# Three transformer blocks on one core: the two halves of the tokens run half a stage apart, and the split weights go through DRAM

## The chip, the cores and the metric

The kernel runs on one core of a Trainium2 chip. The metric is the time of the whole program on the device in microseconds, as the median of repeated runs. Beside it there is one execution that was profiled, whose trace the rows below come from.

## What is computed

512 tokens of 1024 channels go through three blocks in fp32, ten stages in all:

```python
x = first_block(x, c, ...)    # swiglu, hybrid mixer (gMLP + forgetting attention), swiglu, each modulated by c
x = second_block(x, ...)      # swiglu, RWKV-7 recurrence + 31-tap convolution, swiglu
x = third_block(x, ...)       # twice: mixer (top-256 attention + differential attention), swiglu
```

A swiglu is `(silu(h @ w_gate) * (h @ w_up)) @ w_down` with an inner width of 2816. Every mixer begins with projections `h @ w_in` and ends with `@ w_out`. Before each stage stands an RMS norm; in the first two blocks another stands behind it.

## The kernel before, in words

**Halves.** The tokens are two halves of 256, `hf` 0 and 1. Each stage is written out for half 0 and then for half 1 (line 1479). Channels lie on partitions. The second half needs the first half's keys, values, running sums and recurrent state of the same mixer, and nothing else of it.

**Weights.** fp32 products are made of three fp16 matmuls (`three`, line 382). A weight slot is 128 x 1024 fp32, eight 128 x 128 tiles. `Weights.slot` (line 356) loads it by SP into one of three staging buffers `st`, ScalarE writes the high half into a ring buffer `wr`, VectorE the rest (lines 360 to 363). The ring has 12 buffers. A slot is split once and read by both halves: `W(name)` (line 377) keeps one object per matrix, so the buffer is free again when the second half has used it. There are 524 slots. A slot feeds 24 matmuls of 256 columns in each half; the projections to token rows use tile `pt` with 512 columns.

**Order.** The order on every engine is fixed when the program is built. A list scheduler takes, among what is ready, the smallest priority number. That number is a virtual time per half, `vt[hf]`, which `adv` (line 267) advances by each piece's TensorE time, plus `lag[hf]`. The first half has lag 0; the second has `LAGS` of the stage (16 to 30 us), set in its norm (line 451). `boost` makes work earlier, `later` makes it later; attention is boosted by 80 us. The lag is in one half's own TensorE time.

**Stages.** A feed-forward (`ffn`, line 510) makes 22 groups of 16 tiles for gate and up (tile `pgu`, 1056 matmuls a half), then a down-projection of 8 groups (tile `po`, 528). Mixer 1 (line 686) and mixer 3 (line 1227) have projections `pp`, softmax tiles `ps` and an output `po<-mix`. Mixer 2 (line 858) has a recurrence in four chunks: `correction` (line 1057) is a chain of products in tile `pT`, `chunk` (line 1090) a chain through `pA`, `pxy`, `pu` and `psp`; the second half starts from the state that the first leaves. Convolution taps run on VectorE beside it (line 941). The modulation of block one is summed on VectorE from w_ada (`ada_row`, line 558), beside the first feed-forwards.

**GpSimd** clears 20 buffers (`hl`, line 645) and issues no transfer.

Of the kernel before, what the change touches and what calls it, by code (L numbers as in the profile page):

```python
# [243 lines left out]
def tile_three_blocks(ctx: ExitStack, tc: tile.TileContext, d, col_at, con_at, out, phases=None):  # L244
# [107 lines left out]
    class Weights:  # L352
        def __init__(self, name):
            self.name, self.src, self.have = name, d[name], {}

        def slot(self, s):
            if s not in self.have:
                with boost(CB if self.name == "gu10" and s < 3 else WBS.get(self.name, WB)):
                    st = stage.tile([128, 1024], F32, name="st", tag="st")
                    nc.sync.dma_start(out=st, in_=self.src[s])  # L360
                    r = ring.tile([128, 2, 1024], F16, name="wr", tag="wr")
                    S.activation(r[:, 0], st, AF.Copy, scale=WS)  # L362
                    V.scalar_tensor_tensor(r[:, 1], st, WS, r[:, 0], op0=OP.mult, op1=OP.subtract)  # L363
                self.have[s] = r
            return self.have[s]
# [10 lines left out]

    def W(name):
        if name not in weights:
            weights[name] = Weights(name)
        return weights[name]  # L380

# [128 lines left out]
    def ffn(hf, gu, dn, pre, bias, post, key):  # L510
        hh = prenorm(hf, pre, bias, key)
        acts = []
        for n in range(NF):
            adv(hf, 5.23)
            if n % 2 == 0:
                acts.append(m2k(hf, [128, 2, 2, TH], F16, "act"))
            act = acts[-1]
            p = pmm(hf, [128, 2, TH], name="pgu")
            gemm(p[:, 0], W(gu), 16 * n, KD, pair(hh))
            gemm(p[:, 1], W(gu), 16 * n + 8, KD, pair(hh), bank=False)  # L520
            with boost(EB):
                t = t1k(hf, name="fth")
                S.activation(t, p[:, 0], AF.Tanh, scale=0.5 / WS)  # L523
                V.scalar_tensor_tensor(t, t, 1.0, p[:, 0], op0=OP.add, op1=OP.mult)  # L524
                a = t1k(hf, name="fac")
                V.scalar_tensor_tensor(a, t, 0.5 / WS / WS / AS, p[:, 1], op0=OP.mult, op1=OP.mult)  # L526
                split(hf, act[:, 0, n % 2], act[:, 1, n % 2], a)
            beside(key, hf, n)
        x = lambda k: (acts[k // 2][:, 0, k % 2], acts[k // 2][:, 1, k % 2])
        if post is None:  # L530
            out_add(hf, W(dn), NF, x, AS / WS)
# [7 lines left out]
        acc = out_tiles(hf, W(dn), NF, x, y, AS / WS, key)  # L539
        postnorm(hf, acc, y, post)  # L540

# [144 lines left out]
    def mixer1(hf):  # L686
# [24 lines left out]
        for j in range(8):  # L711
            adv(hf, 2.6)
            p = pmm(hf, [128, TH], name="pp")
            gemm(p, W("m1_qk"), (j + 4) % 8 * KD, KD, px)
            with boost(MB):
# [31 lines left out]
        for tt in range(2):  # L747
            vt_ = kv2k(hf, name="v")
            token_gemm(hf, W("m1_v"), hh, tt, lambda p: S.activation(vt_, p, AF.Copy, scale=1.0 / WS))
            m1["v", hf].append(vt_)  # L750
# [26 lines left out]
        for j in range(4):  # L777
            adv(hf, 2.6)
            p = pmm(hf, [128, TH], name="pp")
            gemm(p, W("m1_u"), j * KD, KD, px)  # L780
            if j % 2 == 0:
# [8 lines left out]
        for tt in range(2):  # L790
            g = m2k(hf, name="vg")

            def ev(p, g=g):
                for q in range(2):
                    gelu(hf, g[:, q * 256:(q + 1) * 256], p[:, q * 256:(q + 1) * 256])
            token_gemm(hf, W("m1_g"), hh, tt, ev)
            bn = tiny(hf, 6, "bn")
# [35 lines left out]
        y = lambda m: ys[m // 2][:, m % 2]  # L833
        acc = out_tiles(hf, W("m1_o"), KD, pair(mix), y, 1.0 / WS)
        postnorm(hf, acc, y, one_col(gpost, 8))
# [22 lines left out]
    def mixer2(hf):  # L858
# [36 lines left out]
        for j in order:  # L895
            adv(hf, 2.6)
            p = pmm(hf, [128, TH], name="pp")
            gemm(p, W("m2_s"), j * KD, KD, px)
            with boost(BOOST["m2r"]):
# [19 lines left out]
        def gate_units(j):  # L919
            adv(hf, 5.2)  # L920
            p = pmm(hf, [128, 2, TH], name="pgl")
            gemm(p[:, 0], W("m2_c"), 16 * j, KD, px)
            gemm(p[:, 1], W("m2_c"), 16 * j + 8, KD, px, bank=False)
            with boost(GB):
# [294 lines left out]
        y = lambda m: ys[m // 2][:, m % 2]  # L1219
        acc = out_tiles(hf, W("m2_o"), KD, lambda k: (mix[:, k, 0], mix[:, k, 1]), y, 1.0 / WS)  # L1220
        postnorm(hf, acc, y, lambda k: col("mpost2", k))
# [5 lines left out]
    def mixer3(hf, l):  # L1227
# [24 lines left out]
        def rotated(w, i0, dst, tab, scale):  # L1252
            adv(hf, 2.6)
            p = pmm(hf, [128, TH], name="pp")
            gemm(p, W(w), i0 * KD, KD, px)
            with boost(RB):
# [83 lines left out]
        for tt in range(2):  # L1340
            t = kv2k(hf, name="vb")
            token_gemm(hf, W(f"m3_vb{l}"), hh, tt, lambda p: S.activation(t, p, AF.Copy, scale=1.0 / WS))
            vb.append(t)
# [38 lines left out]
        for tt in range(2):  # L1382
            t = kv2k(hf, name="va")
            token_gemm(hf, W(f"m3_va{l}"), hh, tt, lambda p: S.activation(t, p, AF.Copy, scale=1.0 / WS))
            va.append(t)
# [3 lines left out]
        with boost(BOOST["m3a"]):  # L1389
# [19 lines left out]
        out_add(hf, W(f"m3_o{l}"), KD, pair(mix), 1.0 / WS)  # L1409

# [90 lines left out]
```

## Time and profile before

| | us |
|---|---|
| median of 3 runs (3500.28 to 3503.44) | 3501.31 |
| the profiled execution | 3507.87 |
| its span, first to last instruction | 3506.0 |
| TensorE busy | 3309.1 (94%) |
| VectorE busy | 2171.3 (62%) |
| ScalarE busy | 1545.5 (44%) |

The 16 DMA engines moved 327.89 MB, a mean of 94 GB/s; 28.1% of their time went to the loads' queue. The mean granted TensorE clock was 0.98 of full speed. Stages can be told in the trace by the names of tiles: mixer 1 lies between about 336 and 720 us of the span, mixer 2 between 1320 and 1860, the two layers of mixer 3 between 2100 and 2520 and between 2760 and 3180; each stretch has some feed-forward work of its neighbours in it. A count of matmuls can be short by a few, since some records are missing.

### The profile page before, as it was taken

To read this page: it belongs to the slowest core of one execution; us is meant where nothing else is said; L and a number is where in the kernel's file an instruction comes from. 1 tells how busy PE (TensorE), PEld (TensorE's weight loads), DVE (VectorE), ACT (ScalarE), POOL (GpSimd) and SP (SyncE) were. 2 spreads that over 40 slices of the span, in tenths; PEclk is the share of its full clock that TensorE was granted. 3 is DMA by queue.
4 is the path that set the end of the run, shared out by engine and by line. 5 is a ranking of instruction groups with operands and counts; after the bars stand their busy time and mean duration, and the time that the engine had idled before them with its cause. 6 is when DMAs were issued, how large, how long until landed. Compare 5 with 4: busy or idle time off the path is not lost. (4 is left out here: it accounts for less than half of the span.)

```text
span 3506.0 us, 71986 instructions
## 1 busy us (share of the span) xinstructions
PE 3309.1 (94%) x30164; PEld 2815.7 (80%) x30164; DVE 2171.3 (62%) x5240; ACT 1545.5 (44%) x3335; POOL 19.1 (1%) x24
## 2 busy tenths in 40 slices
PE   5999999999999999997789999889999998999998
PEld 5888867788888888886678887667888876688887
DVE  8953768844374437688884438887544488855433
ACT  3332466433343324424243326886433278853331
POOL 0000000000000000000000000000000000000000
PEclk9999999999999999987889999999999999999999
DMA  8932313232323332201023323112233321123331
GB/s 276 326 110 91 118 55 130 67 103 97 99 96 102 104 97 91 70 5 34 4 89 104 102 97 99 55 43 67 85 104 102 105 85 51 41 80 109 103 99 47
DMA packets 105591, 327.89 MB, mean 94 GB/s; under 512 B 12584, under 2 KB 18088, under 8 KB 105008
## 3 DMA queue, kind: packets, MB, share of 16 engines
q1 hardware_dynamic: 105264, 323.28, 28.1%
q8 instruction: 236, 3.87, 0.5%
q14 instruction: 91, 0.75, 0.1%
HBM read 321.14 MB, written 2.10 MB: 92 GB/s over the span
## 5 line engine op out<-in xcount | busy, mean ns | idle before, releaser
L314 PEld LDWEIGHTS <-wr 128*128 128x128 f16 x24000 | 2351.0, 99 | 327.8 <-issue 25.5
L314 PE MATMUL pgu<-hh,wr 128*128 128x256 f16 x12672 | 1402.6, 273 | 7.9 <-ACT wr L362 2.3
L363 DVE SCALAR_TENSOR_TENSOR wr<-st,wr 128x1024 f16<-128x1024 f32 x524 | 640.3, 1223 | 353.3 <-ACT wr L362 344.0
L314 PE MATMUL po<-act,wr 128*128 128x256 f16 x6336 | 702.0, 273 | 0.1
L362 ACT ACTIVATE wr<-st 128x1024 f16<-128x1024 f32 x524 | 552.2, 1055 | 323.2 <-PE pgu L314 128.3
L314 PE MATMUL pp<-hh,wr 128*128 128x256 f16 x3072 | 384.1, 274 | 4.8 <-DVE rot L1261 2.2
L523 ACT ACTIVATE fth<-pgu 128x256 f32<-128x256 f32 x264 | 101.3, 384 | 590.4 <-PE pgu L314 590.2
L524 DVE SCALAR_TENSOR_TENSOR fth<-fth,pgu 128x256 f32<-128x256 f32 x264 | 111.0, 420 | 355.9 <-ACT fth L523 355.8
L314 PE MATMUL po<-mix,wr 128*128 128x256 f16 x1536 | 198.0, 282 | 15.9 <-ACT mix L444 9.0
L444 ACT ACTIVATE act<-fac 128x256 f16<-128x256 f32 x264 | 110.2, 417 | 174.1 <-DVE fac L526 173.8
L314 PE MATMUL pt<-wr,hh 128*128 128x512 f16 x576 | 145.4, 383 | 1.6 <-DVE wr L363 1.6
L445 DVE TENSOR_TENSOR act<-fac,act 128x256 f16<-128x256 f32 x264 | 111.3, 422 | 50.5 <-ACT act L444 50.0
L492 DVE TENSOR_TENSOR acc<-acc,sq 128x256 f32<-128x256 f32 x84 | 35.4, 421 | 149.5 <-ACT sq L491 149.5
L1260 ACT ACTIVATE rsw<-pp 32x256 f32<-32x256 f32 x304 | 114.3, 376 | 19.6 <-PE pp L314 15.3
L432 ACT ACTIVATE sq<-x 128x256 f32<-128x256 f32 x154 | 56.5, 411 | 134.0 <-DVE x L501 129.6
L526 DVE SCALAR_TENSOR_TENSOR fac<-fth,pgu 128x256 f32<-128x256 f32 x264 | 110.8, 420 | 7.7
L485 ACT ACTIVATE y<-po 128x256 f32<-128x256 f32 x64 | 24.5, 383 | 204.8 <-PE po L314 204.7
L941 DVE SCALAR_TENSOR_TENSOR mix<-glu,cols,mix 128x256 f32<-128x256 f32 x240 | 102.2, 477 | 0.1
L314 PEld LDWEIGHTS <-hh 128*128 128x128 f16 x768 | 62.2, 100 | 48.3 <-issue 3.2
L619 DVE TENSOR_REDUCE amx<-ps 128x1 f32<-128x128 f32 (+3 forms) x160 | 77.3, 487 | 34.4 <-PE ps L314 32.6
L565 DVE SCALAR_TENSOR_TENSOR ada<-adw,csil,ada 128x512 f32<-128x512 f32 x126 | 91.0, 747 | 5.8 <-DMA adw<-in_w_ada_dram 5.6
L501 DVE SCALAR_TENSOR_TENSOR x<-po,x 128x256 f32<-128x256 f32 x64 | 26.9, 422 | 108.1 <-PE po L314 108.0
(356 smaller groups left out, 2935.6 us busy)
## 6 DMA issues: line engine op xcount, KB each, us to landing
st<-in_gu_dram SPq DMA_DIRECT2D x264, 512.0 KB, 3.5
st<-in_dn_dram SPq DMA_DIRECT2D x132, 512.0 KB, 3.5
adw<-in_w_ada_dram SPq DMA_DIRECT2D x144, 256.0 KB, 5.2
st<-in_m_o_dram SPq DMA_DIRECT2D x32, 512.0 KB, 3.6
st<-in_m_b_dram SPq DMA_DIRECT2D x16, 512.0 KB, 3.6
st<-in_m_a_dram SPq DMA_DIRECT2D x16, 512.0 KB, 3.8
st<-in_m_s_dram SPq DMA_DIRECT2D x14, 512.0 KB, 3.6
st<-in_m_qk_dram SPq DMA_DIRECT2D x8, 512.0 KB, 4.0
```

The source lines that it names most:

```text
L314: return PE.matmul(out_, lhsT=l, rhs=r, start=start, stop=stop, skip_group_check=True)
L362: S.activation(r[:, 0], st, AF.Copy, scale=WS)
L363: V.scalar_tensor_tensor(r[:, 1], st, WS, r[:, 0], op0=OP.mult, op1=OP.subtract)
L444: S.activation(hi, src, AF.Copy)
L445: V.tensor_tensor(lo, src, hi, op=OP.subtract)
L523: S.activation(t, p[:, 0], AF.Tanh, scale=0.5 / WS)
L524: V.scalar_tensor_tensor(t, t, 1.0, p[:, 0], op0=OP.add, op1=OP.mult)
L526: V.scalar_tensor_tensor(a, t, 0.5 / WS / WS / AS, p[:, 1], op0=OP.mult, op1=OP.mult)
L565: V.scalar_tensor_tensor(ada_acc[g, h], src, csil[:, k:k + 1], ada_acc[g, h], op0=OP.mult, op1=OP.add)
L619: V.tensor_reduce(nm, s[:, :nk], axis=AX.X, op=OP.max, negate=True)
L941: V.scalar_tensor_tensor(cc(j), gl[:, i:i + TH], dw[:, j * 31 + i:j * 31 + i + 1], cc(j), op0=OP.mult, op1=OP.add)
L1260: S.activation(sw[a:a + 32], p[c:c + 32], AF.Copy, scale=scale)
```

## The change

The lag of the second half becomes 90 us in every stage but the first, whose lag grows by 8 us with each of the eight groups of its down-projection (`WIDEN`). Since a slot can't wait so long in the ring, each half has its own object for a matrix: the first half splits a slot as before, and GpSimd stores the split slot (512 KB, 4 KB a row) to a DRAM buffer `aw...` of its own; the second half loads it by SP from there straight into a ring buffer, without staging and without splitting. `gu10` alone, the first gate and up, is shared as before (`TOGETHER`). The modulation sums of group 8 use the other half's buffers.

```diff
-LAGS = {"f10": 26, "m1": 16, "f11": 22, "f21": 26, "m2": 22, "f22": 24,
-    "m30": 30, "f30": 22, "m31": 30, "f31": 18}
+LAGS = {"f10": 26, "m1": 90, "f11": 90, "f21": 90, "m2": 90, "f22": 90,
+    "m30": 90, "f30": 90, "m31": 90, "f31": 90}
+WIDEN = {"f10": 8}
+TOGETHER = ("gu10",)
...
+    away = pool("away", 1, space=bass.MemoryType.DRAM)
...
+        def __init__(self, name, before=None):
+            self.name, self.src, self.have, self.kept, self.before = name, d[name], {}, {}, before
...
+                    if self.before:
+                        r = ring.tile([128, 2, 1024], F16, name="wr", tag="wr")
+                        nc.sync.dma_start(out=r, in_=self.before.kept[s])
+                    else:
+                        st = stage.tile([128, 1024], F32, name="st", tag="st")
+                        nc.sync.dma_start(out=st, in_=self.src[s])
+                        r = ring.tile([128, 2, 1024], F16, name="wr", tag="wr")
+                        S.activation(r[:, 0], st, AF.Copy, scale=WS)
+                        V.scalar_tensor_tensor(r[:, 1], st, WS, r[:, 0], op0=OP.mult, op1=OP.subtract)
+                        if self.name not in TOGETHER:
+                            self.kept[s] = away.tile([128, 2, 1024], F16, name=f"aw{self.name}_{s}")
+                            nc.gpsimd.dma_start(out=self.kept[s], in_=r)
...
+    def W(name, hf):
+        key = name, hf if name not in TOGETHER else 0
+        if key not in weights:
+            weights[key] = Weights(name, weights[name, 0] if key[1] else None)
+        return weights[key]
...
             beside(key, hf, NF + m)
+            if hf and key in WIDEN:
+                lag[1] += WIDEN[key]
             adv(hf, nk * 0.327)
...
-            ada_acc[g, h] = kv2k(0, name="ada")
+            ada_acc[g, h] = kv2k(g // 8, name="ada")
```

The built order moves with it. On SP, where block one's last feed-forward (`gu11`, `dn11`) is followed by block two's first (`gu21`), the loads stood like this before:

```order
L360 DMA st_10030<-in_dn11_dram 128x1024
L360 DMA st_10059<-in_dn11_dram 128x1024
L360 DMA st_10093<-in_dn11_dram 128x1024
L360 DMA st_10122<-in_dn11_dram 128x1024
L360 DMA st_12230<-in_gu21_dram 128x1024
L360 DMA st_12259<-in_gu21_dram 128x1024
```

and now:

```order
L370 DMA st_10423<-in_dn11_dram 128x1024
L370 DMA st_10454<-in_dn11_dram 128x1024
L370 DMA st_12696<-in_gu21_dram 128x1024
L370 DMA st_12727<-in_gu21_dram 128x1024
L370 DMA st_12766<-in_gu21_dram 128x1024
L367 DMA wr_10621<-awgu11_0_8157 128x2048
L367 DMA wr_10647<-awgu11_1_8188 128x2048
```

All 66 slots of the first half's stage are loaded, then three of its next stage, then all 66 of the second half's stage from the kept copies, then the rest of the first half's next stage. On TensorE the first half's 1056 gate and up matmuls and 301 of its down-projection stand ahead of the second half's first gate matmul, in each of the five stages with kept gate and up weights; between them stand 12 + 192 (`m1_g`, `m1_o`), 254 (`dn11`), 62 + 192 (`m2_c`, `m2_o`), 14 + 192 and 11 + 192 (mixer 3) matmuls of the second half's stage before, with 44, 8, 759, 243 and 243 small ones.

On TensorE at the end of the first half's recurrence in mixer 2 (`psp` and `pxy` of its last chunk), before, `pT<-zb` being the second half's first correction:

```order
L314 MATMUL psp<-uv,bkt 64x64 x8
L314 MATMUL pxy<-uv,aat 64x64 x7
L314 MATMUL pw<-low,wau 128x128
L314 MATMUL pw<-kr,masks 128x128
L314 MATMUL pw<-low,gup 128x256 x2
L314 MATMUL pw<-low,wau 128x128
L314 MATMUL pw<-low,gup 128x256 x2
L314 MATMUL pw<-low,wau 128x128
L314 MATMUL pw<-kr,masks 128x128
L314 MATMUL pT<-zb 64x64 x6
```

and now:

```order
L317 MATMUL psp<-uv,bkt 64x64 x8
L317 MATMUL pxy<-uv,aat 64x64 x7
L317 MATMUL pw<-low,gup 128x256 x4
L317 MATMUL nst<-ones,acc 128x2 x2
L317 MATMUL nbc<-ndg,ones 128x128 x2
L1207 MATMUL pch<-ident,yt 128x128 x6
L317 MATMUL nst<-ones,acc 128x2 x2
L1207 MATMUL pch<-ident,yt 128x128 x2
L317 MATMUL pmu<-csum,ones 128x256
L317 MATMUL nbc<-ndg,ones 128x128 x2
L317 LDWEIGHTS wr
L317 MATMUL po<-mix,wr 128x256
```

Before, the second half's chain follows at once, with no dense matmul between the two chains; now 1096 dense matmuls stand between them. Within the first chain there were 156 by the trace and by the order, and there are 94; within the second 168, and there are 252.

On GpSimd the memsets of `hl` had the queue to themselves; now 480 stores stand there, and the memsets among them:

```order
L376 DMA awdn_20_2828<-wr 128x2048
L376 DMA awdn_21_2859<-wr 128x2048
L661 MEMSET hl 64x1024 x2
L376 DMA awm_qk_5033<-wr 128x2048
L376 DMA awm_qk_5069<-wr 128x2048
```

A store waits for the split of its slot, and for the eighth store ahead of it.

## Rows read from the trace of the kernel before

**Rows 1.** The page, its first line and part 1: busy us, share, instructions.

```profile
span 3506.0 us, 71986 instructions
PE 3309.1 (94%) x30164; PEld 2815.7 (80%) x30164; DVE 2171.3 (62%) x5240; ACT 1545.5 (44%) x3335; POOL 19.1 (1%) x24
```

**Rows 2.** Busy time in stretches of the span, by engine; clock, DMA share, GB/s.

```profile
core 0: us, PE busy (x) PEld busy (x) DVE busy (x) ACT busy (x) POOL busy (x), PEclk, DMA share, GB/s
336.00:720.00 384.00, 366.57 (x3027) 293.22 (x3026) 270.64 (x767) 199.87 (x462) 3.78 (x4) 0.99 0.29 93
960.00:1080.00 120.00, 115.21 (x1042) 101.83 (x1040) 80.22 (x199) 47.10 (x91) 0.00 (x0) 1.00 0.30 97
1080.00:1320.00 240.00, 239.94 (x2197) 214.58 (x2196) 97.16 (x150) 78.35 (x129) 0.00 (x0) 1.00 0.31 98
1320.00:1860.00 540.00, 484.71 (x5395) 403.18 (x5394) 418.52 (x1237) 213.34 (x481) 0.00 (x0) 0.91 0.16 51
2100.00:2520.00 420.00, 382.31 (x3147) 300.83 (x3145) 327.12 (x900) 289.72 (x736) 7.57 (x8) 0.98 0.21 67
2760.00:3180.00 420.00, 387.88 (x3264) 309.68 (x3262) 311.61 (x837) 282.23 (x713) 7.57 (x8) 1.00 0.22 71
```

**Rows 3.** The same stretches, matmuls on split weights (tile wr) alone.

```profile
336.00:720.00 384.00, 300.55 (x2371) 0.99 0.29 93
960.00:1080.00 120.00, 111.26 (x1010) 1.00 0.30 97
1320.00:1860.00 540.00, 284.19 (x2351) 0.91 0.16 51
2100.00:2520.00 420.00, 301.43 (x2275) 0.98 0.21 67
2760.00:3180.00 420.00, 310.65 (x2408) 1.00 0.22 71
```

**Rows 4.** The same stretches, 512-column matmuls into tile pt alone.

```profile
336.00:720.00 384.00, 47.10 (x192) 0.99 0.29 93
2100.00:2520.00 420.00, 49.57 (x192) 0.98 0.21 67
```

**Rows 5.** Stretches inside mixer 2, all engines; columns as in rows 2.

```profile
1485.00:1600.00 115.00, 110.08 (x1613) 91.89 (x1613) 91.22 (x266) 30.15 (x68) 0.00 (x0) 0.87 0.02 7
1600.00:1725.00 125.00, 110.78 (x1606) 90.28 (x1604) 106.80 (x299) 46.98 (x114) 0.00 (x0) 0.90 0.08 25
1725.00:1790.00 65.00, 35.96 (x223) 27.77 (x223) 59.44 (x191) 27.95 (x67) 0.00 (x0) 0.68 0.24 75
```

**Rows 6.** The same three stretches, matmuls on split weights alone.

```profile
1485.00:1600.00 115.00, 21.36 (x156) 0.87 0.02 7
1600.00:1725.00 125.00, 26.76 (x170) 0.90 0.08 25
1725.00:1790.00 65.00, 28.48 (x193) 0.68 0.24 75
```

**Rows 7.** The page, part 5: the two instructions that split a weight slot.

```profile
L363 DVE SCALAR_TENSOR_TENSOR wr<-st,wr 128x1024 f16<-128x1024 f32 x524 | 640.3, 1223 | 353.3 <-ACT wr L362 344.0
L362 ACT ACTIVATE wr<-st 128x1024 f16<-128x1024 f32 x524 | 552.2, 1055 | 323.2 <-PE pgu L314 128.3
```

**Rows 8.** Busy time in the stretch that loads the modulation weights; columns as in rows 2.

```profile
100.00:180.00 80.00, 80.00 (x736) 71.89 (x734) 73.18 (x130) 24.45 (x44) 0.00 (x0) 1.00 0.92 315
```

**Rows 9.** DMA issues: count, KB each, median us from issue to landing.

```profile
st<-in_gu_dram SPq DMA_DIRECT2D x264, 512.0 KB, 3.5
adw<-in_w_ada_dram SPq DMA_DIRECT2D x144, 256.0 KB, 5.2
out_dram<-x SPq DMA_DIRECT2D x16, 128.0 KB, 2.1
maskc<-in_consts_dram SPq DMA_DIRECT2D x1, 128.0 KB, 7.0
```

More of the change, by code (lines that the diff above doesn't have):

```diff
@@ L358, in slot @@
                 with boost(CB if self.name == "gu10" and s < 3 else WBS.get(self.name, WB)):
[L359 to L363, printed above, removed]
+                    if self.before:
[10 more added lines that the diff above has]
+                            nc.gpsimd.dma_start(out=self.kept[s], in_=r)
                 self.have[s] = r
@@ L375, in tile_three_blocks @@
     weights = {}
[L377 to L380, printed above, removed]
+    def W(name, hf):
[3 more added lines that the diff above has]
+        return weights[key]
     def three(out_, a, b, first, last, guard):
@@ L518, in ffn @@
             p = pmm(hf, [128, 2, TH], name="pgu")
-            gemm(p[:, 0], W(gu), 16 * n, KD, pair(hh))
-            gemm(p[:, 1], W(gu), 16 * n + 8, KD, pair(hh), bank=False)
+            gemm(p[:, 0], W(gu, hf), 16 * n, KD, pair(hh))
+            gemm(p[:, 1], W(gu, hf), 16 * n + 8, KD, pair(hh), bank=False)
             with boost(EB):
@@ L530, in ffn @@
         if post is None:
-            out_add(hf, W(dn), NF, x, AS / WS)
+            out_add(hf, W(dn, hf), NF, x, AS / WS)
             return
@@ L538, in y @@
             return yb[0][:, m]
-        acc = out_tiles(hf, W(dn), NF, x, y, AS / WS, key)
+        acc = out_tiles(hf, W(dn, hf), NF, x, y, AS / WS, key)
         postnorm(hf, acc, y, post)
@@ L713, in mixer1 @@
             p = pmm(hf, [128, TH], name="pp")
-            gemm(p, W("m1_qk"), (j + 4) % 8 * KD, KD, px)
+            gemm(p, W("m1_qk", hf), (j + 4) % 8 * KD, KD, px)
             with boost(MB):
@@ L748, in mixer1 @@
             vt_ = kv2k(hf, name="v")
-            token_gemm(hf, W("m1_v"), hh, tt, lambda p: S.activation(vt_, p, AF.Copy, scale=1.0 / WS))
+            token_gemm(hf, W("m1_v", hf), hh, tt, lambda p: S.activation(vt_, p, AF.Copy, scale=1.0 / WS))
             m1["v", hf].append(vt_)
@@ L779, in mixer1 @@
             p = pmm(hf, [128, TH], name="pp")
-            gemm(p, W("m1_u"), j * KD, KD, px)
+            gemm(p, W("m1_u", hf), j * KD, KD, px)
             if j % 2 == 0:
@@ L795, in ev @@
                     gelu(hf, g[:, q * 256:(q + 1) * 256], p[:, q * 256:(q + 1) * 256])
-            token_gemm(hf, W("m1_g"), hh, tt, ev)
+            token_gemm(hf, W("m1_g", hf), hh, tt, ev)
             bn = tiny(hf, 6, "bn")
@@ L833, in mixer1 @@
         y = lambda m: ys[m // 2][:, m % 2]
-        acc = out_tiles(hf, W("m1_o"), KD, pair(mix), y, 1.0 / WS)
+        acc = out_tiles(hf, W("m1_o", hf), KD, pair(mix), y, 1.0 / WS)
         postnorm(hf, acc, y, one_col(gpost, 8))
@@ L897, in mixer2 @@
             p = pmm(hf, [128, TH], name="pp")
-            gemm(p, W("m2_s"), j * KD, KD, px)
+            gemm(p, W("m2_s", hf), j * KD, KD, px)
             with boost(BOOST["m2r"]):
@@ L921, in gate_units @@
             p = pmm(hf, [128, 2, TH], name="pgl")
-            gemm(p[:, 0], W("m2_c"), 16 * j, KD, px)
-            gemm(p[:, 1], W("m2_c"), 16 * j + 8, KD, px, bank=False)
+            gemm(p[:, 0], W("m2_c", hf), 16 * j, KD, px)
+            gemm(p[:, 1], W("m2_c", hf), 16 * j + 8, KD, px, bank=False)
             with boost(GB):
@@ L1254, in rotated @@
             p = pmm(hf, [128, TH], name="pp")
-            gemm(p, W(w), i0 * KD, KD, px)
+            gemm(p, W(w, hf), i0 * KD, KD, px)
             with boost(RB):
@@ L1341, in mixer3 @@
             t = kv2k(hf, name="vb")
-            token_gemm(hf, W(f"m3_vb{l}"), hh, tt, lambda p: S.activation(t, p, AF.Copy, scale=1.0 / WS))
+            token_gemm(hf, W(f"m3_vb{l}", hf), hh, tt, lambda p: S.activation(t, p, AF.Copy, scale=1.0 / WS))
             vb.append(t)
@@ L1383, in mixer3 @@
             t = kv2k(hf, name="va")
-            token_gemm(hf, W(f"m3_va{l}"), hh, tt, lambda p: S.activation(t, p, AF.Copy, scale=1.0 / WS))
+            token_gemm(hf, W(f"m3_va{l}", hf), hh, tt, lambda p: S.activation(t, p, AF.Copy, scale=1.0 / WS))
             va.append(t)
@@ L1408, in mixer3 @@
                 to_channels(hf, yas[qt], mix, 0, qt, None)
-        out_add(hf, W(f"m3_o{l}"), KD, pair(mix), 1.0 / WS)
+        out_add(hf, W(f"m3_o{l}", hf), KD, pair(mix), 1.0 / WS)
     def finish(hf):
```

4 lines of the change are left out of this document (1 added, 3 removed).

## Prediction

> **What bounds the kernel now.** I read the page's first part, then the span in stretches, then the same stretches with one kind of matmul alone, and last the DMA rows. TensorE is busy 94% of 3506.0 us, VectorE 62%, ScalarE 44% [rows 1]. So at most the other 6% can be won by rearranging, and a little more where TensorE is busy but badly filled. In a stretch with both halves in feed-forward work there is nothing to win: 2197 matmuls fill 239.94 of 240 us, 0.109 us each, and the DMA engines are busy 0.31 of the time [rows 2]. The reader is to hold the mixers against that price. With 0.109 us for each matmul on split weights, and twice that for a 512-column one, the dense work of a mixer stretch is known, and what is left is small matmuls and waiting [rows 2 to 4]:
> - mixer 1: 384 - (2371 + 192) x 0.109 = 105 us (the 192 wide ones are among the 2371 and count once more)
> - mixer 2: 540 - 2351 x 0.109 = 284 us
> - mixer 3, first layer: 420 - (2275 + 192) x 0.109 = 151 us; second layer, with as many wide ones, 420 - (2408 + 192) x 0.109 = 137 us
>
> TensorE shows no busy time for 17, 55, 38 and 32 us of these. The granted clock has a mean of 0.91 in mixer 2 (part of it at 1.2 GHz, the rest at 2.4) and 0.98 to 1.00 in the others [rows 2].
>
> **The change, part by part.** The run is summed against the profiled execution, 3507.87 us with 3506.0 us of span; the median of the three runs, 3501.31 us, is 6.6 us lower, and the forecast is shifted by that.
>
> *Splitting.* 524 slots are split by ScalarE and VectorE before and after, 1.055 and 1.223 us each [rows 7]. Nothing is added there; only the time of day changes. The modulation sums that move to the other half's buffers cost 0: same instructions, and they lie beside feed-forward work that leaves VectorE idle more than half the time [rows 2].
>
> *Mixer 2.* Its recurrence is a chain of small products. In the kernel before, the first half's chain takes about 115 us and holds 156 dense matmuls, the second's 125 us and 170, the tail behind 65 us and 193 [rows 5, 6]. Less the dense work, 17, 18.5 and 21 us, this leaves 98, 106 and 44 us. The order after has 94 dense matmuls in the first chain (one half's down-projection has run out), 252 in the second (gate and up of the first half), and 1096 between the chains where there were none. A chain is bound by its own steps: VectorE is busy 91 of 115 and 107 of 125 us, TensorE waits among them. So I leave the two chains at 98 and 106 us, take 34 of the tail's 44 us away because ready weights now stand behind it, and add 8 us to the second chain for the first half's splits in it (252/24 = 10.5 slots x 1.223 = 13 us on an engine that has 18 us free). That is -26 us. The bounds are -104 us, all of mixer 2's idle time (55 us) and its low clock (9% of 540, 49 us), and +10 us.
>
> *Mixers 1 and 3.* The second half's attention now stands beside the first half's gate and up matmuls, and the first half's beside the second's down-projection. VectorE and ScalarE, busy 0.78 and 0.69 of the first mixer 3 stretch and 0.70 and 0.52 of mixer 1 [rows 2], get a longer stretch for the same work. I take four fifths of the 87 us without TensorE work, -70 us; the bounds are 0 and -105 us (the idle time and a fifth more for matmuls that now fill the pipe).
>
> *Between two feed-forward stages*, 120 us hold 1010 matmuls, 110 us [rows 2, 3]. Half of the 10 us goes: -5 us.
>
> *The DMA engines.* 480 slots (all but the 44 of the first gate and up) are written out, 0.524 MB each, and 480 read back instead of being reused. In the order the halves don't alternate slot by slot: each time the first half runs its 1056 gate and up matmuls and 301 of the down-projection before the second half's first gate matmul. These 1357 matmuls need 56.5 slots, 29.6 MB in and 29.6 MB out. In the stage after mixer 1 the second half adds 192 matmuls (8 slots, 4.2 MB) and 44 small ones: 63.4 MB in 1549 x 0.109 + 44 x 0.13 = 175 us, 362 GB/s (0.13 us: the 113 us that 872 other matmuls take, their pipe waits with them, in the first mixer 3 stretch, 382.31 - 268.9 over 3147 - 2275). One stage later it adds 254 (5.5 MB): 64.8 MB in 176 us, 368 GB/s. The most that the trace shows is 315 GB/s at a DMA share of 0.92, that is 342 GB/s at a share of 1 [rows 8]. At 342 these stages take 185 and 189 us: +10 and +13 us, +23 us. In the two stages beside mixer 3's attention, 243 small matmuls at 0.13 us stretch 63.7 MB over 202 us, 315 GB/s; beside mixer 2 it is less. These cost 0 as long as a store costs the engines what a load does. No store of this size is in the trace. From below: 128 KB stored lands in 2.1 us where a load of 128 KB took 7.0 us in the crowded start, so a store may cost nothing extra [rows 9]; from above, see the slower rival. I take the load's price, the nearest row in size.
> The Trainium skill, DMA: Bandwidth & Descriptors, "Where 436 GB/s comes from", gives two higher limits for a core, about 358 GB/s at the HBM side and 435 GB/s at the ports. By the first the +23 us would be about +7 us, by the second 0; the measured 342 GB/s is a load phase in which VectorE, too, was busy 73 of 80 us, so it may be low.
>
> *Waits that are added.* A slot is free only when its store has landed. A load lands in 3.5 us [rows 9], its split takes 2.3 us [rows 7], the store some 3.5 us more: 9.3 us for a slot, against 12 slots x 2.6 us = 31 us of matmuls in the ring. Three staging buffers give a slot every (3.5 + 2.3)/3 = 1.9 us, under the 2.6 us that TensorE needs; at the 5.2 us that loads took in the crowded start [rows 9] it is 2.5 us, just enough. So 0 us, with little to spare. SP and POOL issue in order: a load that waits for a slot holds the next half's loads, and a memset of a head buffer that waits holds the stores behind it. Both wait for work that the order puts ahead of them, so 0 to 2 us for each of ten memset pairs; I take 0.
>
> Sum: -26 - 70 - 5 + 23 = -78 us, 3430 us for the profiled execution, **3423 us** as a median. Its own range is 3360 to 3480 us.
>
> **The rivals.**
> *All waiting goes* (12%). For it: dense work is always at hand by priority, and 142 us are idle. Against it: only 94 dense matmuls stand in the first chain. Then 17 + 55 + 38 + 32 + 49 + 5 = 196 us go and the DMA engines cost nothing: 3312, as a median 3305 us.
> *The halves alternate but the mixers gain nothing* (15%). The order runs one half's stage after the other's rather than both at once, so it hardly does what it says: with one half's attention at a time fewer tiles are in flight, and its softmax steps are waited for. Then 20 us of gain in the mixers and 5 us between stages meet 23 us: 3506, median 3499 us.
> *The DMA engines become the bound* (23%), the slower one. For it: the demand is already at 342 GB/s in two stages, and the price of a store is not in the trace. A store that takes the engines 1 + e times a load's time adds 29.6e MB to each stage: 87e us in the two tight ones, and in the two of 202 us whatever passes them (186 + 87e - 202). At e = 0.32 the 101 us of gain are eaten up (23 + 55 + 23): that is where it decides. At e = 0.5 the cost is 23 + 87 + 55 = 165 us instead of 23: 3430 + 142, median 3565 us. Against it: the 2.1 us of the small store.
> The Trainium skill, DMA: Bandwidth & Descriptors, "Issuing engines are not separate DMA queues", speaks for it: a transfer issued from GpSimd runs on the same 16 engines as one from SP, so the second queue brings no bandwidth. The kernel before has one such queue in use, and no run so far shows two.
>
> **How the numbers follow.** Forecast 50%, rivals 12, 15 and 23%. A measurement of this kernel can tell about 0.2%, 7 us, from no change. Faster than 3494 us: the forecast, the first rival and a third of the second, 67%. Within 7 us: 8% of the second. Slower: the third and the rest, 25%. The range of 8 in 10 is 3330 to 3550 us: it leaves out the lower two thirds of the first rival (8%) and the half of the third that lies above it (12%).
>
> **What would show it.** Right: in the mixer 2 stretch two chains of 110 to 130 us each, with a dense stretch of some 120 us between them and no tail; TensorE idle time in mixers 1 and 3 under 25 us in all; DMA share above 0.9 while the first half runs alone, with ScalarE's split waiting for its load. Wrong: a DMA share of 0.9 or more over the whole of each feed-forward pair with TensorE idle in it; TensorE waiting for loads of kept slots; stores that land in more than 15 us; a chain shorter than 100 us, which would mean it was not bound by its own steps.

## The result, and the profile after

The changed kernel takes 3863.15 us (median of 4, 3857.49 to 3864.38) against 3502.38 us: 1.1019 of the kernel before, 95% interval 1.0991 to 1.1047. It is 10% slower; 3423 us were forecast, in a range of 3330 to 3550 us.

The page of the changed kernel: its first line, busy time (us, share, instructions), DMA queues (packets, MB, share of 16 engines) and DMA issues (count, KB, median us to landing).

```profile
span 3855.6 us, 74364 instructions
PE 3398.3 (88%) x30156; PEld 2830.8 (73%) x30164; DVE 2170.9 (56%) x5240; ACT 1541.7 (40%) x3335; POOL 275.8 (7%) x504
...
q1 hardware_dynamic: 174384, 574.97, 47.2%
q0 software_dynamic: 69120, 251.69, 16.0%
...
st<-in_gu_dram SPq DMA_DIRECT2D x264, 512.0 KB, 5.3
awgu<-wr POOLq DMA_DIRECT2D x220, 512.0 KB, 6.2
wr<-awgu SPq DMA_DIRECT2D x220, 512.0 KB, 3.4
st<-in_dn_dram SPq DMA_DIRECT2D x132, 512.0 KB, 6.4
```

VectorE and ScalarE do the same work as in [rows 1]. TensorE is idle for 3855.6 - 3398.3 = 457 us instead of 197, and its busy time has grown by 89 us for the same matmuls. 260 + 89 = 349 us is the difference of the two spans. The mean granted clock, a mix of 1.2 and 2.4 GHz, fell from 0.98 to 0.959, which is an estimated 3309.1 x 0.98 / 0.959 - 3309.1 = 72 of the 89 us; in the rows below it is 0.88 where TensorE was busy 85.55 of 115 us, and 1.00 where it was busy 119.29 of 120. A staged load lands in 5.3 to 6.4 us where it took 3.5 [rows 9].

Busy time in stretches of the changed kernel, columns as in [rows 2], all engines. In order: the first half's gate and up matmuls beside the second half's attention of mixer 1; the first half's feed-forward ahead of mixer 2; first chain, dense stretch and second chain of mixer 2; the second half's last feed-forward.

```profile
660.00:740.00 80.00, 60.43 (x464) 45.58 (x463) 37.30 (x64) 26.48 (x39) 10.67 (x20) 0.94 0.76 246
1140.00:1320.00 180.00, 150.09 (x1313) 129.12 (x1311) 104.02 (x179) 76.55 (x120) 28.85 (x54) 0.96 0.92 317
1620.00:1735.00 115.00, 85.55 (x1387) 71.82 (x1384) 104.20 (x292) 35.75 (x79) 3.21 (x6) 0.88 0.22 77
1735.00:1900.00 165.00, 148.60 (x1275) 120.25 (x1274) 92.89 (x272) 64.36 (x145) 9.09 (x17) 0.96 0.57 192
1900.00:2030.00 130.00, 112.45 (x1604) 91.44 (x1603) 111.50 (x305) 46.20 (x98) 5.34 (x10) 0.92 0.24 79
3660.00:3780.00 120.00, 119.29 (x1090) 106.27 (x1088) 30.41 (x82) 15.66 (x39) 0.00 (x0) 1.00 0.62 207
```

The same with matmuls on split weights alone, columns as in [rows 3]:

```profile
660.00:740.00 80.00, 60.43 (x464) 0.94 0.76 246
1140.00:1320.00 180.00, 147.70 (x1297) 0.96 0.92 317
1620.00:1735.00 115.00, 12.39 (x81) 0.88 0.22 77
1735.00:1900.00 165.00, 134.67 (x1119) 0.96 0.57 192
1900.00:2030.00 130.00, 37.53 (x252) 0.92 0.24 79
3660.00:3780.00 120.00, 118.27 (x1082) 1.00 0.62 207
```

A second half that only reads kept slots runs at 120/1082 = 0.111 us a matmul, nearly the dense price of 0.109 us. A first half that loads, splits and stores runs at 180/1297 = 0.139 us, a slot every 3.3 us instead of 2.6; beside mixer 1's attention at 80/464 = 0.172 us, a slot every 4.1 us.

What ScalarE does in 15 us of the second stretch, in order of time (start us, us, what, then the idle time before it and what ended it):

```profile
1200.03 1.06 ACT L372 ACTIVATE wr<-st 128x1024 f16<-128x1024 f32 x1 [1.29 <-DMA st<-in_gu_dram]
...
1203.65 1.06 ACT L372 ACTIVATE wr<-st 128x1024 f16<-128x1024 f32 x1 [2.26 <-DMA st<-in_gu_dram]
1206.43 1.06 ACT L372 ACTIVATE wr<-st 128x1024 f16<-128x1024 f32 x1 [1.73 <-DMA st<-in_gu_dram]
...
1208.79 1.06 ACT L372 ACTIVATE wr<-st 128x1024 f16<-128x1024 f32 x1 [0.75 <-DMA st<-in_gu_dram]
...
1212.40 1.06 ACT L372 ACTIVATE wr<-st 128x1024 f16<-128x1024 f32 x1 [2.29 <-DMA st<-in_gu_dram]
```

Every split waits for its load, four splits in 12.37 us, 3.1 us each. That is the staging loop: a staging buffer is taken for the load (a median of 6.4 us between 1140 and 1320 us), the two halves of the split (2.3 us) and a hand-over of 0.1 us, and three buffers give a slot every third of it, 2.9 us. ScalarE runs in order, so tanh, squares and evictions behind such a split wait with it.

What ended ScalarE's and TensorE's waits (us in total, times, longest), first over the stretch 1140 to 1320 us (ScalarE), then over the whole run (TensorE), and last the two norm waits of TensorE over the whole run before:

```profile
ACT wr L372 <- DMA awgu<-wr: 30.1, 14, 3.7
ACT wr L372 <- DMA st<-in_dn_dram: 25.0, 14, 2.8
ACT wr L372 <- DMA st<-in_gu_dram: 20.6, 12, 2.9
```

```profile
PE pgu L317 <- DMA wr<-awgu: 46.5, 14, 10.7
PE nbc L317 <- DVE ndg L435: 40.0, 25, 7.8
PE pgu L317 <- DVE wr L373: 33.3, 47, 1.0
PE nst L317 <- DVE acc L447: 31.1, 12, 6.7
PE pgu L317 <- ACT wr L372: 26.7, 20, 2.8
```

```profile
PE nbc L314 <- DVE ndg L421: 33.4, 32, 7.7
PE nst L314 <- DVE acc L433: 19.9, 20, 6.3
```

A split waits for its load or for the store of an older slot in its ring buffer, and TensorE for the split or for a kept slot. The norm waits (`nbc`, `nst`) were there before, 53 us against 71. The waits for slots are new, as the pages show for the gate and up matmuls, before and after (us busy, mean ns, then idle time before them):

```profile
L314 PE MATMUL pgu<-hh,wr 128*128 128x256 f16 x12672 | 1402.6, 273 | 7.9 <-ACT wr L362 2.3
```

```profile
L317 PE MATMUL pgu<-hh,wr 128*128 128x256 f16 x12672 | 1499.0, 279 | 122.7 <-DMA wr<-awgu 46.5
```

To say where the time went, I cut each run into stages at the same counts of matmuls on split weights (in the order they start, a 512-column one counted twice; cuts at 2940, 4900, 10780, 12740, 14700, 17640, 19600, 22540 of 25152) and took from each stage's time 0.109 us for each. What is left, in us:

| | 1st FF | mixer 1 | 2 FF | mixer 2 | FF | mixer 3 | FF | mixer 3 | last FF | sum |
|---|---|---|---|---|---|---|---|---|---|---|
| before | 64 | 99 | 18 | 278 | 0 | 151 | 0 | 137 | 9 | 757 |
| after | 76 | 145 | 136 | 281 | 48 | 191 | 31 | 168 | 31 | 1107 |
| no stores (e2) | 76 | 103 | 54 | 257 | 23 | 158 | 9 | 150 | 14 | 843 |
| two rings (e5) | 104 | 118 | 44 | 238 | 32 | 135 | 18 | 130 | 11 | 830 |
| lag alone (e12) | 66 | 103 | 35 | 245 | 20 | 135 | 18 | 127 | 11 | 759 |
| all buffers (e13) | 86 | 104 | 35 | 229 | 25 | 135 | 18 | 128 | 11 | 771 |

219 us of the loss lie in the feed-forward stretches behind the first (118 + 48 + 31 + 22), where only 27 us were to be won, and 117 us in mixers 1 and 3.

### The profile page after: what moved, and what is told of

Read it like the earlier page. It is cut to its first block, busy times and chain, and to the rows that moved or that the text cites. A ratio compares the mean times of both kernels' runs of the same rounds, so it can differ in the third digit from the quotient of the medians.

```text
span 3855.6 us, 74364 instructions
## 1 busy us (share of the span) xinstructions
PE 3398.3 (88%) x30156; PEld 2830.8 (73%) x30164; DVE 2170.9 (56%) x5240; ACT 1541.7 (40%) x3335; POOL 275.8 (7%) x504
## 3 DMA queue, kind: packets, MB, share of 16 engines
q1 hardware_dynamic: 174384, 574.97, 47.2%
q0 software_dynamic: 69120, 251.69, 16.0%
## 4 chain that ended last, share of the span: by engine, by line
PE 36%; issue 32%; DMA 14%; DVE 9%; ACT 7%; POOL 2%; ACTq 0%; POOLq 0%; SPq 0%; DVEq 0%
PE pgu L317 17%; PE po L317 10%; DMA st<-in_gu_dram 4%; DMA st<-in_dn_dram 3%; DVE wr L373 3%; ACT wr L372 3%; PE ps L317 2%; DMA st<-in_m_o_dram 1%; PE pp L317 1%; DMA wr<-awgu 1%; ACT rsw L1276 1%; DMA awgu<-wr 1%; PE pT L317 1%; POOL awgu L376 1%; PE pxy L317 1%
## 5 line engine op out<-in xcount | busy, mean ns | idle before, releaser
L317 PE MATMUL pgu<-hh,wr 128*128 128x256 f16 x12672 | 1499.0, 279 | 122.7 <-DMA wr<-awgu 46.5
L317 PE MATMUL po<-act,wr 128*128 128x256 f16 x6336 | 737.9, 274 | 24.4 <-DVE fac L542 12.7
L376 POOL DMA_DIRECT2D awgu<-wr x220 | 117.7, 535 | 1355.5 <-DVE wr L373 393.6
L317 PE MATMUL po<-mix,wr 128*128 128x256 f16 x1536 | 183.5, 280 | 6.3 <-ACT mix L458 3.1
L376 POOL DMA_DIRECT2D awdn<-wr x132 | 70.7, 535 | 636.3 <-DVE wr L373 381.8
L446 ACT ACTIVATE sq<-x 128x256 f32<-128x256 f32 x154 | 58.0, 412 | 135.0 <-DVE x L517 122.7
```

Source lines behind the costliest of these rows:

```text
L317: return PE.matmul(out_, lhsT=l, rhs=r, start=start, stop=stop, skip_group_check=True)
L376: nc.gpsimd.dma_start(out=self.kept[s], in_=r)
```

## The experiments

Theories after the result: the **staging loop** (three buffers are too few once a load lands in 6 us), the **DMA engines** (their throughput is the end of it), and the **order** (the halves run one after the other, whatever the lags). Ratios are to the kernel before on the same chip, with 95% intervals. It took 3495 to 3507 us in the several sets of runs, so a difference between runs of two sets is taken from their ratios, times 3502 us.

### More staging, no stores, the old lags, splitting twice

e1_five_stages, as many bytes on chip:

```diff
-RING = 12
+RING = 10
-    stage = pool("stage", 3)
+    stage = pool("stage", 5)
```

> Five staging buffers and ten ring buffers instead of three and twelve, the same bytes on chip. Staging loop (three buffers, each busy for a load of 6.2 us, a split of 2.3 us and 0.5 us of hand-over, give a slot only every 3.0 us where TensorE wants one every 2.6 us): the loop would give a slot every 1.8 us, so the stretches in which the first half runs alone come down to the dense price and some 200 us of the loss go, about 3660 us. DMA engines (full at about 330 GB/s): loads that are issued earlier only land later, the landing time rises towards 10 us and the slot period stays; 3830 to 3880 us. Order (the halves run one after the other and VectorE and ScalarE stand behind splits): within 40 us of 3863 us.

Measured 3808.15 us, ratio 1.0901 (1.0869 to 1.0932): 41 us of the loss come back, not 200. Stretches of this run, columns as in [rows 2]:

```profile
820.00:840.00 20.00, 19.37 (x175) 16.96 (x174) 13.90 (x30) 11.16 (x18) 4.26 (x8) 1.00 1.02 418
...
880.00:900.00 20.00, 20.00 (x186) 17.92 (x184) 9.76 (x11) 8.49 (x11) 4.26 (x8) 1.00 1.03 419
...
820.00:900.00 80.00, 76.98 (x698) 68.12 (x697) 60.76 (x120) 43.18 (x71) 15.44 (x29) 1.00 0.95 370
...
1140.00:1320.00 180.00, 158.54 (x1380) 135.76 (x1379) 105.01 (x182) 78.27 (x122) 28.76 (x54) 0.96 0.89 332
```

Where slots are to be had, the engines move 419 GB/s of loads and stores together while TensorE runs at full pace (186 matmuls in 20.00 us). Over 80 us they move 370 GB/s. So 342 GB/s is no limit, though a share of 1.03 suggests that little is left above 419. The engines' theory was right in that loads of the down-projection land later, in 9.0 us instead of 6.4. Three staging buffers were too few, but that is the smaller part, net of the two ring buffers given up for it.

e2_no_stores:

```diff
-                        if self.name not in TOGETHER:
+                        if self.name == "dn10":
...
-                        nc.sync.dma_start(out=r, in_=self.before.kept[s])
+                        k = weights["dn10", 0].kept
+                        nc.sync.dma_start(out=r, in_=k[s if self.name == "dn10" else s % len(k)])
```

> Only the 22 slots of dn10 are stored, and the second half reads its other slots from these 22 copies: 458 of 480 stores (240 MB) are gone, the loads, their sizes and the order stay; the second half's weights are wrong from mixer 1 on. DMA engines: with the stores gone a stretch of the first half asks for 200 GB/s instead of 400, the feed-forward stretches come down to the dense price, and 200 to 250 us go: 3610 to 3660 us. Staging loop: loads land in 3.3 us again, a slot every 2.0 us, the same 200 to 250 us. Order: whatever is then left above 3502 us is the order's; by it alone the time would stay above 3800 us.

Measured 3594.65 us, ratio 1.029 (1.026 to 1.032). The stores cost 255 us in this order (0.0729 x 3502), seven tenths of the loss. A staged gate-and-up load lands in 3.8 us without them.

e3_old_lags has `LAGS` of the kernel before and no `WIDEN`, the rest as in the change.

> The lags of the kernel before (16 to 30 us, none widened), all stores and reads of kept slots as in the change. Staging loop: a new slot is wanted only every 5.2 us, so the loop has room even at 6.2 us a load; 3500 to 3530 us. DMA engines: three transfers of 0.524 MB in 5.2 us are 302 GB/s in every feed-forward stretch, just under what the engines gave; 3510 to 3620 us. Order: with the order of before back, within 30 us of 3502 us.

Measured 3839.31 us, ratio 1.099 (1.0944 to 1.1036). All three theories missed. With lags of 16 to 30 us the time is nearly that of 90 us, and the built order says why: SP still loads 41 + 22 slots of the first half's feed-forward, then all 66 of the second half's. A ring buffer is given out in the order in which the program's text asks for it, a stage of the first half ahead of the same stage of the second, and the list scheduler can't pass that: the second half's first slot needs a buffer that comes 66 turns after the first half's first one. The lags had set the order only while both halves used one slot.

e4_split_twice has no stores: the second half loads fp32 again and splits again (`if False:` in place of `if self.before:`).

> The lags of the change, no stores: the second half loads its slots in fp32 again and splits them again (480 more splits of 1.055 us on ScalarE and 1.223 us on VectorE). DMA engines and staging loop: as without stores, 3610 to 3660 us, plus what the 587 us more on VectorE cost in the mixers, where it is busy 0.8 of the time (about 200 of the slots fall there, up to 100 us). Order: above 3800 us.

Measured 3722.19 us, ratio 1.0655 (1.057 to 1.0739): 128 us above e2. VectorE's busy time is 2720.2 us instead of 2170.6, and by the same cuts as above mixers 1, 2 and 3 are 23, 15, 44 and 44 us over e2, the feed-forward stretches within 3 us of it or below. Splitting again is cheaper than storing here, and still costs.

### A ring for each half

e5_two_rings:

```diff
-RING = 12
+RING = 6
...
                     if self.before:
-                        r = ring.tile([128, 2, 1024], F16, name="wr", tag="wr")
+                        r = ring.tile([128, 2, 1024], F16, name="wr", tag="wr1")
```

> The change with a ring of 6 buffers for each half instead of one of 12 for both; lags, stores and loads as in the change. Ring order (one ring is given out in the order of the program's text, all of a stage's first-half slots before its second-half slots, whatever the lags): with two rings the halves' matmuls do alternate, a new slot is wanted every 5.2 us instead of 2.6, the traffic of a feed-forward pair is spread to 300 GB/s, and at least half of the 230 us lost in the feed-forward stretches comes back: 3600 to 3700 us. DMA engines alone: the same bytes as evenly spread ask for 300 of the 330 GB/s that they gave at best; they stay the bound where the mixers' small matmuls do not thin the demand: 3700 to 3800 us. Staging loop: as the ring order, 3550 to 3650 us.

Measured 3587.49 us, ratio 1.0214 (1.0138 to 1.0289). 282 us come back with every store, load and lag in place; the time lies just under the range expected of the ring's order, and in that of the staging loop. SP's loads of a feed-forward pair now alternate, one to three of the first half, then one to three kept slots (from 1076 us on). A stretch of this run, columns as in [rows 2]:

```profile
1220.00:1320.00 100.00, 100.00 (x918) 89.62 (x917) 37.56 (x56) 30.84 (x52) 9.58 (x18) 1.00 0.84 294
```

918 matmuls in 100 us is the dense price, with all the traffic of the change running beside it at 294 GB/s. Its staged gate-and-up loads land in 5.4 us, no sooner than in the change; a slot is wanted only every 5.2 us, and the loop gives that.

e6_two_rings_no_stores is e5 with e2's edit.

> The same two rings, and only the 22 slots of dn10 stored, the second half reading its other slots from these copies (its weights are wrong from mixer 1 on): what the alternation of the halves alone is worth, with 200 GB/s asked for. If half a stage of lag is worth what was forecast for the mixers (96 us of gain), 3400 to 3430 us; if the chains of mixer 2 and the attention are bound by their own steps, 3480 to 3560 us. The difference to the run with two rings and stores is the price of the stores when their traffic is spread.

Measured 3532.09 us, ratio 1.0069 (1.0042 to 1.0097). Four runs stand in a square: one ring 1.1019 with stores and 1.029 without, two rings 1.0214 and 1.0069. The stores cost 255 us with one ring and 51 us with two; one ring costs 77 us without stores and 282 with them. So neither alone is the cause: some 200 us come only where the two meet. And with the stores gone the lag still wins nothing.

e7_two_rings_old_lags is e5 with e3's lags.

> Two rings of 6, all stores and reads of kept slots, the lags of the kernel before: the traffic alone in an order that is nearly that of the kernel before. Ring order: the halves alternate by ten groups of 24 matmuls, so what is lost against 3495 us is the traffic's own price, 20 to 100 us. DMA engines: as e5 with less to gain in the mixers, 3700 to 3800 us.

Measured 3616.74 us, ratio 1.0297 (1.0233 to 1.0361), 29 us slower than with 90 us of lag, though the two intervals overlap. With two rings the lags do set the order: mixer 2 has 293 us beyond the dense price (278 before), against 238 in e5, and the feed-forward stretches behind mixers 2 and 3 have 1 and 0 us (0 and 0 before), against 32 and 18.

e11_two_rings_five_stages is e5 with `RING = 5` and five staging buffers.

> Two rings of 5 and five staging buffers instead of two rings of 6 and three, the same bytes; stores, loads and lags as in the change. Two rings without stores took 3532 us, with them 3587 us. If those 55 us are the landing times (5 to 6 us a load against three staging buffers), most of them come back: 3540 to 3565 us. If they are the 16 engines' throughput at 300 GB/s, or buffers that stores hold longer, 3580 to 3620 us, since the rings are shorter.

Measured 3534.42 us, ratio 1.0087 (1.0057 to 1.0118): 44 of the 51 us. The loads land no sooner (5.5 us), five buffers hide it.

e12_lag_alone is e6 with the shared gate and up slots of the first feed-forward in both rings:

```diff
-                        r = ring.tile([128, 2, 1024], F16, name="wr", tag="wr")
+                        r = ring.tile([128, 2, 1024], F16, name="wr", tag=("wr", "wr1")[s % 2] if self.name in TOGETHER else "wr")
                         S.activation(r[:, 0], st, AF.Copy, scale=WS)
```

> Two rings of 6, no stores but dn10's 22 (the second half reads its other slots from these copies, its weights are wrong from mixer 1 on), and the shared first gate and up slots use both rings in turn, so that the first feed-forward has 12 buffers as before: what half a stage of lag is worth with the split weights for nothing. If the forecast of the mixers was right (96 us), 3410 to 3450 us. If the attention and the chains are bound by their own steps, what mixers 2 and 3 win is lost where a stage begins: 3490 to 3520 us.

Measured 3503.67 us, ratio 0.9997 (0.9973 to 1.0022). Half a stage of lag without the stores is worth nothing: TensorE is idle for 3507.7 - 3317.7 = 190 us instead of 197. The second half still loads 480 slots, but no wait of TensorE for one stands in this run's trace.

e13_all_buffers is e11 with e12's edit, all 480 stores and 480 reads in it.

> Two rings of 5, five staging buffers, the shared first gate and up slots use both rings in turn; all 480 stores and 480 reads, and the lags, as in the change. If the change lost its time to buffers (staging, ring order, short rings in the first feed-forward) and not to the engines' throughput: the 3534 us of two rings with five staging buffers less the 29 us that the two rings in turn gave without stores, 3500 to 3515 us, no different from the kernel before. If the traffic itself costs, 3520 to 3540 us.

Measured 3530.08 us, ratio 1.0085 (1.0064 to 1.0106). 327 of the 357 us are gone by arrangement of the same 15 buffers, without a byte less. But the time lies in the range that was expected if the traffic itself costs, not in that for buffers alone: the edit that won 25 us without stores (e6 to e12) wins nothing here against e11. 31 us to e12 stay, and the profiled runs show 12 of them (3520.0 and 3507.7 us of span): in the table, 20 us in the first feed-forward, where only 5 of the added stores lie, and nothing lost elsewhere on balance. The shared ring has 10 buffers there instead of 12, but that this is the cause isn't shown (e14, with 7, has 76 us there). So the traces show no share of the engines' throughput once the halves alternate and the loop is deep enough; what the other 19 us are stays open.

### Output slots that wait in the ring

In the change, eight slots of `m1_o` for the second half stand in the one ring ahead of the first half's next gate and up slots. SP's issues of them in the changed kernel (start, us, what), and TensorE's first use:

```profile
602.02 12.14 SPq L367 DMA_DIRECT2D wr<-awm_o  x4
...
646.81 0.33 SPq L367 DMA_DIRECT2D wr<-awm_o  x1
```

```profile
789.04 3.22 PE L317 MATMUL po<-mix,wr 128*128 128x256 f16 x28
```

They hold 8 of 12 buffers for over 140 us. What that does is seen in ScalarE's splits, first the longest wait between 660 and 740 us (us in total, times, longest), then in order of time:

```profile
ACT wr L372 <- DMA awgu<-wr: 33.7, 9, 6.2
```

```profile
693.44 1.06 ACT L372 ACTIVATE wr<-st 128x1024 f16<-128x1024 f32 x1 [2.48 <-DMA awgu<-wr]
...
697.74 1.06 ACT L372 ACTIVATE wr<-st 128x1024 f16<-128x1024 f32 x1 [2.94 <-DMA awgu<-wr]
```

Here no split waits for its load. It waits for the store of the split before last: the stores issued at 688.26 and 692.23 us land at 693.37 and 697.59, and a split starts 0.1 us behind each. So two buffers take turns, each held for about 8 us (split 2.3, hand-over 0.4, store 5.2), a slot every 4.1 us. The remaining two probably held the slots of the second half's last projections, which run until 733 us; that is not shown. e8_outputs_apart and e14_outputs_apart_five take them out of the common ring:

```diff
-RING = 12
+RING = 8
...
-                        r = ring.tile([128, 2, 1024], F16, name="wr", tag="wr")
+                        o = self.name.endswith("_o") or self.name[:4] == "m3_o"
+                        r = ring.tile([128, 2, 1024], F16, name="wr", tag="wo" if o else "wr", bufs=4 if o else RING)
                         nc.sync.dma_start(out=r, in_=self.before.kept[s])
```

(e14: `RING = 7`, 3 for the outputs, five staging buffers.)

> The change, one ring for everything except the second half's output projections (m1_o, m2_o, m3_o: 8 slots a mixer), which get a ring of 4 of their own; the common ring shrinks from 12 to 8, the same bytes. Parked slots (in the order of the program these 8 slots stand ahead of the first half's next gate and up slots, and hold 8 of 12 buffers until the second half's attention is done, so 4 buffers, each kept for a split, 24 matmuls and a store of 6 us, feed TensorE meanwhile): the first half's gate and up stretch beside each of the four mixers' attentions comes down towards the price without stores, 20 to 40 us at each, 3720 to 3800 us. Staging loop or DMA engines alone: nothing is gained where the ring is not short, and 8 buffers are fewer than 12 elsewhere: 3850 to 3900 us.

> One common ring of 7, a ring of 3 for the second half's output projections, five staging buffers: the same 10 ring buffers as the run with five staging buffers (3808 us), in which 8 slots of output projections left 2 of 10 to the first half's gate and up beside each attention. Parked slots: TensorE gets a slot every 2.6 to 3.0 us there instead of every 4, some 30 us at each of four mixers, 3690 to 3750 us. A half at a time alone: 3790 to 3850 us, since the common ring is shorter.

Measured 3930.35 us, ratio 1.1201 (1.1142 to 1.1259), and 3869.7 us, ratio 1.1052 (1.1015 to 1.1089): both slower than what they were made from (3863.15 and 3808.15 us), and above every range expected. The time from the end of the first half's output projection of mixer 1 to the start of the second's is 238 us in the change, 243 in e8, 240 in e14. A ring for these slots doesn't pay for the buffers it takes. It doesn't clear the wait either: in e8's common ring of 8, splits still start behind the store of the split before last (33.2 us of such waits between 690 and 770 us), while second-half projections that go through that ring run until 783 us. So the two runs don't show what unused slots in the one ring cost.

### A version with few stores

e9_mixer2_60 and e10_mixer2_90 keep the kernel before everywhere but around mixer 2:

```diff
-TOGETHER = ("gu10",)
+KEPT = ('dn21', 'm2_s', 'm2_c', 'm2_o', 'gu22', 'dn22')
+RING = 6
+LAGS = {'f10': 26, 'm1': 16, 'f11': 22, 'f21': 26, 'm2': 60, 'f22': 60, 'm30': 30, 'f30': 22, 'm31': 30, 'f31': 18}
+WIDEN = {'f21': 4}
...
+                        r = ring.tile([128, 2, 1024], F16, name="wr", tag="wr" if self.name in KEPT else ("wr", "wr1")[next(turn) % 2])
```

(e10: 90 for `m2` and `f22`, and 8 in `WIDEN`.)

> Stores, reads of kept slots and a longer lag (60 us) only around mixer 2: dn21, mixer 2's and the next feed-forward's weights (118 of 480 slots); two rings of 6, which shared matrices use in turn; all other lags as in the kernel before. In the order 179 dense matmuls stand in the first chain of mixer 2 and 270 in the second, and 700 between them. If dense work beside the chains and between them is what pays: 3450 to 3480 us. If the chains are bound by VectorE and what is won behind them is lost again where the lag is given back: 3490 to 3520 us.

> The same with a lag of 90 us in mixer 2 and behind it: 94 and 106 dense matmuls in the chains, 1242 between them. If dense work in the chains pays, 20 to 40 us slower than with 60 us; if the chains are bound by VectorE and only the tail counts, the same within 10 us.

Measured 3514.26 us, ratio 1.0024 (1.0002 to 1.0046), and 3539.39 us, ratio 1.01 (1.0059 to 1.0141). Mixer 2 has 258 and 256 us beyond the dense price against 278 before: 449 dense matmuls in the chains win no more than 200. The feed-forward behind it gives back 15 and 30 us, and mixer 3's first layer 22 and 19. e10 is 27 us slower than e9, as was expected if dense work in the chains paid; the profiled runs (3531.0 and 3521.8 us of span) show 9 of them, and by the stages they lie in the feed-forward behind, not in the chains. No version was found that beats the kernel before.

## Why the prediction was wrong

- **The order.** The prediction read that a first half runs 1357 matmuls alone, and counted its bytes, but didn't ask what sets that order, the lags or the ring. It is the ring (e3, e5, e7). The second rival named it ("it hardly does what it says") and priced only a missing gain, not what a half alone does to the buffers.
- **"So 0 us, with little to spare."** This term, the added waits, is the step that failed first. The sum had three staging buffers giving a slot every 1.9 us, at worst 2.5; the trace shows 3.1 us, since a load lands in a median of 6.4 us beside the stores. The 5.2 us of its worst case were landings of 256 KB loads; the 512 KB loads in the stretch of [rows 8] landed in 4.5 us. It also took all 12 ring buffers as cover, and beside mixer 1's attention two of them took turns. TensorE's idle time ahead of gate and up matmuls alone went from 7.9 to 122.7 us. The stores, priced at +23 us by bandwidth, cost 255 us in this order (e2): in the two stretches looked at, through buffers held longer, staging buffers by later loads and ring buffers by stores.
- **The DMA engines, +23 us.** The limit of 342 GB/s, scaled up from [rows 8], was wrong: in e1 370 GB/s were moved for 80 us and 419 for 20, where 362 and 368 were asked for. By throughput the term would have been about 0, though no run holds such a rate for a whole stage of 175 us; e13 bears it out for 300 GB/s alone. Of the two limits that the Trainium skill gives in DMA: Bandwidth & Descriptors, "Where 436 GB/s comes from", e1's trace passes the lower, 358 GB/s, and stays under the higher, 435.
- **The slower rival** had the side right and the mechanism wrong. A store costs the engines less than a load: 16.0% of their time for 251.69 MB against 47.2% for 574.97 MB, 0.0636 against 0.0821% a MB, so e = -0.23 and not over 0.32. The loads' queue has smaller rows in it too; against what the kept slots alone added to it (47.2% of 3855.6 less 28.1% of 3506.0 us, 835 us for the same bytes) a store's 617 us give -0.26. That a transfer issued from GpSimd shares the 16 engines (the Trainium skill, DMA: Bandwidth & Descriptors, "Issuing engines are not separate DMA queues") fits: loads land in 3.8 us without stores, in 5.3 with them.
- **Mixers 1 and 3, -70 us.** Wrong in sign in the change (+46, +40, +31 us), and without stores and with good buffers (e12) nothing: 103 against 99, 135 + 18 against 151 + 0, 127 + 11 against 137 + 9 (the feed-forward stage behind is added, since small matmuls spill into it). TensorE's idle time there was not waiting for the other half's dense work, which is there in e12 and does not shorten it; four fifths of it was a share chosen without a row for it.
- **Mixer 2, -26 us.** About right as a mechanism. The chains take 115 and 130 us with VectorE busy 104.20 and 111.50, as forecast, and the dense stretch stands between them. By itself (e12) the stage wins 33 us and the next gives 20 back; in the change it wins nothing, and 48 us are lost behind it, 28 of them TensorE idle (between 2027 and 2289 us; by the trace 8.5 for slots and 10.5 for norms) and most of the rest busy time at a granted clock of 0.94.
- **Between feed-forward stages, -5 us.** +17 us even without stores (35 against 18).
- **Right:** splitting costs nothing more in time, and no store waits behind a memset (each is issued within 2 us of its split, 0.4 us at the median). The sign that ScalarE's split waits for its load at a DMA share above 0.9 came (0.92), and so did one for wrong, TensorE waiting for kept slots (46.5 us).

Open stays how the 282 us between one ring and two divide between the doubled pace of a half alone and the buffers that wait in the ring; e8 and e14 left unused slots in the shorter ring and don't tell them apart. No run issues the stores from another engine than GpSimd, so whether their landing time is the store's own or the queue's stays open too.

## What to carry to other kernels

Where a pool hands out buffers in the order of the program's text, that order rules over priorities and lags: look in the built order for which stream the ring lets go first before pricing anything by the schedule. Price a transfer by what it holds (how long a buffer is taken, how many there are, how fast the next is wanted at the fastest moment), not by mean bandwidth over a stage. And give dense work to another engine's idle time only where a row shows that the idle time is waiting for that work; a chain bound by its own steps takes no less with a neighbour.

## What was not expected of the hardware

- Loads and stores together reached 419 GB/s for 20 us at a DMA share of 1.03 and 370 for 80 us at 0.95 (e1), where loads alone had shown 315 at 0.92 [rows 8].
- A store of 512 KB takes the engines about three quarters of a load's time for each byte, yet lands later: 6.2 us against 3.4 us for the same slot read back, and 6.5 us where only 22 slots are stored (e2).
- A staged load lands later with stores beside it at the same rate: 6.4 us at 317 GB/s, against 4.5 us at 315 GB/s of loads alone [rows 8].
- 294 GB/s of traffic beside dense matmuls cost TensorE nothing: 918 in 100.00 us (e5).
